# A fused decoder block: the first branch's q and k chain placed ahead of the second q's sums, both halves of a turned block sent to DRAM before either is read back, and the second branch turned behind the 21st unit

## The chip, the cores and the metric

The kernel runs on one core of a Trainium2 chip. The metric is the time of one execution in microseconds; three runs of the kernel before gave 373.08 (median), 372.19 and 373.63. Engines are called PE (matrix products), DVE (VectorE), ACT (ScalarE), POOL (GpSimd) and SP (it only issues transfers here). Each runs its own instructions in a fixed order and waits for others by semaphores.

## The reference, cut to what matters

One decoder layer on 256 tokens with 1024 channels: two attention branches of eight heads with 64 channels, a gated merge, and a gated convolutional feed-forward part.

```python
h = rms_norm(x, attn_norm_g)
qa, ka, va, qb, kb, vb, f_logit, g_logit = split(h @ w_in)
qa, ka = partial_rope(rms_norm(heads(qa), gqa)), partial_rope(rms_norm(heads(ka), gka))
o_a = softmax(causal(qa @ ka.T / 8)) @ va            # first branch: one block of 256 keys
qb, kb = rms_norm(heads(qb), gqb), rms_norm(heads(kb), gkb)
c = cumsum(log_sigmoid(f_logit + b_forget))
o_b = softmax(causal(qb @ kb.T / 8 + c[t] - c[s])) @ vb   # second branch
x = x + (gate_0 * (o_a @ w_a) + gate_1 * (o_b @ w_b)) @ w_out
u, g = split(rms_norm(x, ffn_norm_g) @ w_up)
x = x + (silu(conv3(g)) * u) @ w_down
```

## The kernel before

Every product is made of three single-pass products of rounded operands: each weight w is split into whi (rounded, ACT, line 137) and wlo = w - whi (DVE, line 138), and x likewise into xh and xl. Weights come in chunks of 1 MB, each issued by SP (line 130) into one of three buffers `raw`; a chunk has two halves, and the split of a half is called a unit here. Eight units belong to the first branch's q and k ("head"). Then follow, by the list `chunks`, units 9 to 12 for the second branch's q, 13 to 16 for its k, 17 and 18 for gate 0, 19 and 20 for gate 1, 21 to 24 for the first branch's v ("qkv", 0), 25 and 26 for gate 2, 27 to 30 for the second branch's v ("qkv", 3), then the other gates, two units each (31 and 32 gate 3, 33 and 34 gate 4, 35 and 36 gate 5). A chunk's load can start when the units of the chunk three places earlier are split, since they share a buffer.

PE's order is written by hand: first q and k (line 285), second q and k (line 299, 11 us each), gate 0, the forget logits, gate 1, the first branch's scores (line 462), the first v, gate 2, the second branch's scores, the second v, gates 3 to 5, the transposes of the probabilities, and so on to the feed-forward part. On the other engines a scheduler sets the order by program order, by priorities (`soon`, FIRST) and by edges `after(i, j)`, which only say that i stands behind j. So such an edge costs nothing of itself, but an instruction that waits holds everything behind it on its engine.

The path of q and k from projection to scores goes over several engines. `finish_qk` squares the projections on ACT, sums on DVE (line 317), takes the inverse root (`rsqrt_mean`, DVE and ACT in turn) and multiplies on DVE (line 329) into `qn` (second branch: into the tile `ol`). For the first branch POOL then turns 16 of each head's channels by the rope (lines 335 to 338). `turn_blocks` transposes 32x32 blocks on DVE (line 353), half d=1 first and then half d=0, which has the rope, and POOL issues a write of each half to DRAM, 512 KB (line 356, `blocks<-pT`). `move_blocks` reads them back in four transfers of 256 KB (line 364, `bias<-blocks`), and ACT scales them into qT and kT (lines 369 and 374; second branch: into the tile `oh`). POOL also works on the forget rows (lines 397, 412 to 415), which end in a sum over time that the second branch's bias (`forget_bias`) needs.

A pool of eight PSUM banks serves all products. The built program lets a product have a bank as soon as its last holder has been read. The sixth bank of the second branch's scores, which their third pair of heads is the first to use, is here the one from which ACT reads the first half of the first v (line 303); the second v has the banks of gate 2, which DVE's product reads (line 581), and of the first v's other half (line 305).

## Time and profile before

| | |
|---|---|
| runs | 373.08 us (372.19 to 373.63) |
| profiled execution, its own time | 373.12 us |
| its span, first to last instruction | 371.3 us |
| PE busy | 354.9 us, 96% of the span |
| DVE, ACT, POOL busy | 277.8, 222.6, 47.1 us |
| mean granted TensorE clock | 0.981 |
| moved by DMA | 72.49 MB, 195 GB/s |

The span is 1.8 us shorter than the time of the same execution; differences of spans stand for differences of times. A row of a timeline has the start and the length in us, engine, line, operation, tiles (written <- read) and shape, how often it came in a row, and in brackets how long the engine idled before it and what ended that. A row of waits has the sum, the count and the longest. A row of DMA issues has the queue, the count, KB of each and the median us from issue to landing, within the window asked for.

### The profile page before, as it was taken

To read this page: it belongs to the slowest core of one execution; us is meant where nothing else is said; L and a number is where in the kernel's file an instruction comes from. 1 tells how busy PE (TensorE), PEld (TensorE's weight loads), DVE (VectorE), ACT (ScalarE), POOL (GpSimd) and SP (SyncE) were. 2 spreads that over 40 slices of the span, in tenths; PEclk is the share of its full clock that TensorE was granted. 3 is DMA by queue.
4 is the path that set the end of the run, shared out by engine and by line. 5 is a ranking of instruction groups with operands and counts; after the bars stand their busy time and mean duration, and the time that the engine had idled before them with its cause. 6 is when DMAs were issued, how large, how long until landed. Compare 5 with 4: busy or idle time off the path is not lost.

```text
span 371.3 us, 7462 instructions
## 1 busy us (share of the span) xinstructions
PE 354.9 (96%) x3053; PEld 337.3 (91%) x3053; DVE 277.8 (75%) x475; ACT 222.6 (60%) x378; POOL 47.1 (13%) x70
## 2 busy tenths in 40 slices
PE   9999996199999999999999999999999999999995
PEld 5888885088889999999999999999999999999995
DVE  5898899585699656986779967677686867778653
ACT  5858660586999599453768645455464555545420
POOL 3532264242013000000170000000000000000000
PEclk9999999589999999999999999999999999999999
DMA  8977548976233843565464566446555545645003
GB/s 286 405 281 251 210 171 286 309 230 248 118 114 115 341 129 112 216 214 190 166 228 145 197 223 211 165 197 227 166 184 219 196 169 203 228 150 192 3 0 115
DMA packets 13347, 72.49 MB, mean 195 GB/s; under 512 B 1880, under 2 KB 3040, under 8 KB 5888
## 3 DMA queue, kind: packets, MB, share of 16 engines
q1 hardware_dynamic: 11664, 66.62, 49.7%
q0 software_dynamic: 1504, 5.38, 4.5%
q8 instruction: 24, 0.39, 0.4%
q14 instruction: 11, 0.09, 0.1%
q10 hardware_dynamic: 144, 0.00, 0.0%
HBM read 68.84 MB, written 3.15 MB: 194 GB/s over the span
## 4 chain that ended last, share of the span: by engine, by line
PE 89%; DMA 5%; POOL 2%; DVE 1%; ACT 1%; issue 1%; POOLq 0%
PE bank L571 14%; PE bank L572 14%; PE bank L573 14%; PE bank L299 9%; PE bank L285 6%; PE bank L784 5%; PE bank L785 5%; PE bank L783 5%; DMA bias<-blocks 3%; DMA blocks<-pT 2%; PE bank L707 2%; PE bank L681 2%; PE bank L709 2%; PE bank L708 2%; PE bank L683 2%; PE bank L682 2%
## 5 line engine op out<-in xcount | busy, mean ns | idle before, releaser
L138 DVE TENSOR_TENSOR wlo<-raw,whi 128x1024 fp32r<-128x1024 f32 x120 | 147.1, 1231 | 49.3 <-ACT whi L137 49.2
L137 ACT ACTIVATE whi<-raw 128x1024 fp32r<-128x1024 f32 x120 | 125.6, 1059 | 79.3 <-PE bank L572 37.1
L573 PE MATMUL bank<-oh,wlo 128*128 128x256 f32 x352 | 96.8, 275 | 0.0
L571 PE MATMUL bank<-oh,whi 128*128 128x256 f32 x352 | 96.8, 275 | 0.0
L572 PE MATMUL bank<-ol,whi 128*128 128x256 f32 x352 | 96.8, 275 | 0.0
L573 PEld LDWEIGHTS bank<-oh,wlo 128*128 128x128 f32 x352 | 66.1, 188 | 0.0
L572 PEld LDWEIGHTS bank<-ol,whi 128*128 128x128 f32 x352 | 66.1, 188 | 0.0
L571 PEld LDWEIGHTS bank<-oh,whi 128*128 128x128 f32 x352 | 66.1, 188 | 0.0
L571 PE MATMUL bank<-xh,whi 128*128 128x256 f32 x128 | 35.7, 279 | 0.0
L572 PE MATMUL bank<-xl,whi 128*128 128x256 f32 x128 | 35.3, 275 | 0.0
L573 PE MATMUL bank<-xh,wlo 128*128 128x256 f32 x128 | 35.3, 275 | 0.0
L571 PEld LDWEIGHTS bank<-xh,whi 128*128 128x128 f32 x128 | 24.0, 188 | 1.0 <-issue 0.4
L572 PEld LDWEIGHTS bank<-xl,whi 128*128 128x128 f32 x128 | 24.0, 188 | 0.1
L573 PEld LDWEIGHTS bank<-xh,wlo 128*128 128x128 f32 x128 | 24.0, 188 | 0.0
L299 PE MATMUL bank<-whi,xh 128*128 128x512 f32 x64 | 21.2, 391 | 0.0
L299 PE MATMUL bank<-whi,xl 128*128 128x512 f32 x64 | 21.0, 388 | 0.0
L299 PE MATMUL bank<-wlo,xh 128*128 128x512 f32 x64 | 21.0, 388 | 0.0
L750 DVE TENSOR_TENSOR sq<-bank,rs 128x512 f32<-128x512 f32 x22 | 15.1, 691 | 6.6 <-PE bank L573 6.5
L681 PE MATMUL bank<-oh,whi 128*128 128x256 f32 x64 | 17.6, 275 | 0.0
L682 PE MATMUL bank<-ol,whi 128*128 128x256 f32 x64 | 17.6, 275 | 0.0
L683 PE MATMUL bank<-oh,wlo 128*128 128x256 f32 x64 | 17.6, 275 | 0.0
L707 PE MATMUL bank<-xh,whi 128*128 128x256 f32 x64 | 17.6, 275 | 0.0
(197 smaller groups left out, 769.0 us busy)
## 6 DMA issues: line engine op xcount, KB each, us to landing
raw<-in_wu SPq DMA_DIRECT2D x22, 1024.0 KB, 4.8
raw<-in_wd SPq DMA_DIRECT2D x11, 1024.0 KB, 4.8
raw<-in_qkv SPq DMA_DIRECT2D x8, 1024.0 KB, 5.3
raw<-in_wg SPq DMA_DIRECT2D x8, 1024.0 KB, 5.2
raw<-in_wb SPq DMA_DIRECT2D x4, 1024.0 KB, 5.5
raw<-in_wo SPq DMA_DIRECT2D x4, 1024.0 KB, 4.8
raw<-in_head SPq DMA_DIRECT2D x6, 512.0 KB, 6.6
blocks<-pT POOLq DMA_DIRECT2D x4, 512.0 KB, 5.4
```

The source lines that it names most:

```text
L137: i = nc.scalar.activation(hi[:, s], raw[:, s], AF.Copy)
L138: d = nc.vector.tensor_tensor(lo[:, s], raw[:, s], hi[:, s].bitcast(F32), op=ALU.subtract)
L285: nc.tensor.matmul(pt[t], lhs[:, k, t * P:(t + 1) * P], rhs, start=(k == 0 and i == 0), stop=(k == KT - 1 and i == 2))
L299: nc.tensor.matmul(pt[t], lhs[:, k, t * P:(t + 1) * P], rhs[:, c], start=(k == 0 and i == 0), stop=(k == KT - 1 and i == 2))
L571: nc.tensor.matmul(o, wh[:, w], mh[:, k], start=(k == 0 and i == 0), stop=False)
L572: nc.tensor.matmul(o, wh[:, w], ml[:, k], start=False, stop=False)
L573: nc.tensor.matmul(o, wl[:, w], mh[:, k], start=False, stop=(k == KT - 1 and i == 1))
L681: nc.tensor.matmul(o, wh[:, w], oh[:, 4 * br + k], start=(k == 0), stop=False)
L682: nc.tensor.matmul(o, wh[:, w], ol[:, 4 * br + k], start=False, stop=False)
L683: nc.tensor.matmul(o, wl[:, w], oh[:, 4 * br + k], start=False, stop=(k == 3))
L707: nc.tensor.matmul(o, wh[:, w], mh[:, k], start=(k == 0 and i == 0), stop=False)
L783: nc.tensor.matmul(o, wh[:, w], ah, start=(p == 0 and h == 0 and c == 0), stop=False)
```

## The change

The first branch's q and k product goes in front of the second q's sums on DVE by an edge on these sums; some splits (units 16 and 18 on DVE, 19, 23 and 27 on ACT) get edges behind steps of q and k's chain; the reads of a turned block stand behind both writes; the second branch's transposition moves from behind gate 1's product to behind unit 21's wlo, and its reads from behind the forget rows of `forget_chain` to behind the first forget row; its scaling on ACT stands behind the second pair's softmax instead of the third's.

```diff
@@ load
+                if (c, h) == (("qkv", 0, 1), 0):
+                    after(i, moved[0])
+                if (c, h) == (("qkv", 3, 0), 0):
+                    after(i, moved[1])
+                if (c, h) in ((("qkv", 2, 1), 1), (("wg", 0), 1)):
+                    after(d, state["qn"])
+                if (c, h) == (("wg", 1), 0):
+                    after(i, state["exp"])
+                if (c, h) == (("qkv", 0, 0), 0):
+                    state["turn"] = d
@@ finish_qk
-                if br and isk:
-                    after(i, state["qn"])
+                if br:
+                    after(i, state["last"][1] if isk else state["qn"])
...
-        rsqrt_mean(f.rearrange("p m t h -> p (m t h)"), ss.rearrange("p m t h -> p (m t h)"), HD, [n * NT * NH], "qfv")
+        state["exp"] = rsqrt_mean(f.rearrange("p m t h -> p (m t h)"), ss.rearrange("p m t h -> p (m t h)"), HD, [n * NT * NH], "qfv")[1]
@@ turn_blocks, move_blocks
-            nc.gpsimd.dma_start(rd[:, c], blocks[:, c])
-        return rd, i
+            sent = nc.gpsimd.dma_start(rd[:, c], blocks[:, c])
+        return rd, i, sent
...
-                if behind is not None:
-                    after(i, behind)
+                after(i, behind)
@@ forget_a
-        nc.vector.tensor_copy(total, fp[0:NH, :S])
+        after(nc.vector.tensor_copy(total, fp[0:NH, :S]), state["turn"])
...
-        nc.gpsimd.tensor_tensor(row(1), total, rsB[:NH], op=ALU.mult)
+        fg["row"] = nc.gpsimd.tensor_tensor(row(1), total, rsB[:NH], op=ALU.mult)
@@ the main sequence
-                rd, i = turn_blocks(0, state["qn"])
-                moved.append(move_blocks(0, rd))
+                rd, i, sent = turn_blocks(0, state["qn"])
+                moved.append(move_blocks(0, rd, sent))
     catch_up(lag=1, lo=state["qn"])
-    gate(0)
+    read = gate(0)
+    after(read, state["qn"])
     with soon():
         flat_lo = forget_a()
+        rd, i, sent = turn_blocks(1, state["turn"])
+        after(fg["row"], sent)
     catch_up(lo=flat_lo)
 
     read = gate(1)
+    after(read, i)
     with soon():
         sps = scores(0)
-        rd, i = turn_blocks(1, state["last"][1])
-        after(i, read)
-        done = softmax(0, 0, sps[0], i)
+        done = softmax(0, 0, sps[0], read)
     forget_chain(done)
     with soon():
-        for pair in (1, 2):
-            softmax(0, pair, sps[pair], i)
-        last = move_blocks(1, rd, fg["z"], last_exp[0])
-        softmax(0, 3, sps[3], i, last)
+        softmax(0, 1, sps[1], read)
+        moved.append(move_blocks(1, rd, fg["row"], last_exp[0]))
+        for pair in (2, 3):
+            softmax(0, pair, sps[pair], read, moved[1])
```

In the built program PE's order and SP's are as before. PSUM banks are given out otherwise in one place: the sixth bank of the second branch's scores is now the one of gate 2, and the second v has both banks of the first v. Lines of the changed kernel are one higher than before at the splits, ten or eleven higher from `finish_qk` on. The first place is DVE, where the first branch's factor (`qf` with 32 elements) is ready to be made. Before:

```order
L230 SCALAR_TENSOR_TENSOR qfv<-qfv 128x32
L317 TENSOR_REDUCE ss<-sq 128x8
L231 TENSOR_TENSOR qfv<-qfv 128x32
L317 TENSOR_REDUCE ss<-sq 128x8
L232 SCALAR_TENSOR_TENSOR qf<-qfv 128x32
L138 TENSOR_TENSOR wlo<-raw,whi 128x1024
L322 TENSOR_TENSOR qf<-qf,rsw 128x32
L228 TENSOR_SCALAR qfv<-ss 128x16
L138 TENSOR_TENSOR wlo<-raw,whi 128x1024
L329 TENSOR_TENSOR qn<-bank,qf 128x2x4x32 x8
```

The two sums (`ss`) are the second q's, and units 16 and 17 are split ahead of qn. The same place on DVE after the change:

```order
L241 SCALAR_TENSOR_TENSOR qfv<-qfv 128x32
L242 TENSOR_TENSOR qfv<-qfv 128x32
L243 SCALAR_TENSOR_TENSOR qf<-qfv 128x32
L333 TENSOR_TENSOR qf<-qf,rsw 128x32
L340 TENSOR_TENSOR qn<-bank,qf 128x2x4x32 x8
L328 TENSOR_REDUCE ss<-sq 128x8 x2
L364 STREAM_TRANSPOSE pT<-qn 128x1024
L239 TENSOR_SCALAR qfv<-ss 128x16
L139 TENSOR_TENSOR wlo<-raw,whi 128x1024
```

The factor and all eight products now stand ahead of the sums, and the splits behind. The second place is POOL's queue from the end of the rope to the second branch's reads. Before:

```order
L356 DMA blocks<-pT 128x1024
L364 DMA bias<-blocks 32x4x512
L356 DMA blocks<-pT 128x1024
L364 DMA bias<-blocks 32x4x512 x3
L397 TENSOR_TENSOR gates<-gates,rsB 8x256
L356 DMA blocks<-pT 128x1024 x2
L412 TENSOR_TENSOR gates<-gates 8x256
L413 TENSOR_TENSOR gates<-gates 8x256
L415 TENSOR_TENSOR gates<-gates 8x256
L364 DMA bias<-blocks 32x4x512 x4
```

One read of half d=1 stands between the two writes of the first branch. POOL after the change:

```order
L367 DMA blocks<-pT 128x1024 x2
L375 DMA bias<-blocks 32x4x512 x4
L367 DMA blocks<-pT 128x1024 x2
L407 TENSOR_TENSOR gates<-gates,rsB 8x256
L375 DMA bias<-blocks 32x4x512 x4
L422 TENSOR_TENSOR gates<-gates 8x256
```

Both writes go first in each branch, and the second branch's reads stand ahead of three forget rows instead of behind them. The third place is ACT around the scaling of the second branch's q and k (`oh<-bias`). Before, with buffer numbers (whi_905 to whi_959 are units 27 to 30, s_872 the fourth pair's probabilities, bank_885 and bank_886 the first v):

```order
L137 ACTIVATE whi_921<-raw_903 128x1024
L137 ACTIVATE whi_939<-raw_937 128x1024
L137 ACTIVATE whi_959<-raw_937 128x1024
L303 ACTIVATE V_179<-bank_885,rsw_175 128x512
L369 ACTIVATE oh_180<-bias_862,gq_174 128x1024
L374 ACTIVATE oh_180<-bias_862,sm_80 128x4x64 x4
L490 ACTIVATE s_872,l_874<-s_872,nm_873 128x128
L490 ACTIVATE s_872,l_874<-s_872,nm_873 128x256
```

Units 27 to 30 and the first copy of v stand ahead of the scaling, and one pair's exponentials behind. ACT after the change:

```order
L420 ACTIVATE gates_79<-gates_79 8x256
L379 ACTIVATE oh_180<-bias_849,gq_174 128x1024
L384 ACTIVATE oh_180<-bias_849,sm_80 128x4x64 x4
L500 ACTIVATE s_859,l_861<-s_859,nm_860 128x128
L500 ACTIVATE s_859,l_861<-s_859,nm_860 128x256
L500 ACTIVATE s_859,l_861<-s_859,nm_860 128x128
L500 ACTIVATE s_859,l_861<-s_859,nm_860 128x256
L500 ACTIVATE s_872,l_874<-s_872,nm_873 128x128
L500 ACTIVATE s_872,l_874<-s_872,nm_873 128x256
L500 ACTIVATE s_872,l_874<-s_872,nm_873 128x128
L500 ACTIVATE s_872,l_874<-s_872,nm_873 128x256
L138 ACTIVATE whi_905<-raw_903 128x1024
```

The scaling moved in front of two pairs' exponentials (s_859 and s_872) and of unit 27 with all that follows it. On DVE the split of that unit stands ahead of gate 2's product, which frees the bank that the second scores wait for:

```order
L504 RECIPROCAL r_870<-l_861 128x4
L504 RECIPROCAL r_883<-l_874 128x4
L139 TENSOR_TENSOR wlo_906<-raw_903,whi_905 128x1024
L591 TENSOR_TENSOR gates_79<-bank_958,rsB_177 128x512
L139 TENSOR_TENSOR wlo_922<-raw_903,whi_921 128x1024
```

Before, gate 2's product stood behind the splits of units 27 to 30.

## The prediction

> **What bounds the kernel now.** I read the page's busy times first, then the list of who waits for whom on PE, then PE's timeline around the one long wait, and last the granted clock in short windows.

> ```profile
> span 371.3 us, 7462 instructions
> PE 354.9 (96%) x3053; PEld 337.3 (91%) x3053; DVE 277.8 (75%) x475; ACT 222.6 (60%) x378; POOL 47.1 (13%) x70
> PE bank L462 <- ACT kT L374: 11.5, 1, 11.5
> 61.15 0.28 PE L573 MATMUL bank<-xh,wlo 128*128 128x256 f32 x1
> 72.92 5.21 PE L462 MATMUL bank<-kT,qT 64*64 64x64 f32 x64 [11.49 <-ACT kT L374]
> 78.06 0.50 PE L299 MATMUL bank<-whi,xh 128*128 128x512 f32 x1
> 94.61 2.41 PE L462 MATMUL bank<-oh 64*64 64x64 f32 x64
> 96.95 0.50 PE L299 MATMUL bank<-whi,xh 128*128 128x512 f32 x1
> 64.00:65.00 1.00, 0.00 (x0) 0.52 0.98 397
> 77.00:78.00 1.00, 1.00 (x20) 0.65 0.49 197
> ```

> PE is busy for 354.9 of 371.3 us and waits for another engine once: 11.49 us, from 61.43 to 72.92, until ACT has written the first branch's kT. Everything else that PE does is back to back, so PE is the bound and this wait is what a better order can win. The wait costs more than itself. The two windows (length, PE busy, granted clock, DMA share, GB/s) show the clock at half from about 64.0, that is 2.6 us after PE fell idle, to about 77.7, 4.8 us after it resumed. So the first branch's 64 score matmuls take 78.06 - 72.92 = 5.14 us where the second branch's take 96.95 - 94.61 = 2.34. The stall is worth 11.49 + 2.80 = 14.3 us.

> **The change, part by part.** *First branch.* These rows are the chain that ends the wait: DVE, POOL, then ACT.

> ```profile
> 36.17 0.18 DVE L230 SCALAR_TENSOR_TENSOR qfv<-qfv 128x32 f32<-128x32 f32 x1
> 38.95 0.69 DVE L317 TENSOR_REDUCE ss<-sq 128x8 f32<-128x512 f32 x1 [2.60 <-ACT sq L316]
> 42.80 2.74 DVE L329 TENSOR_TENSOR qn<-bank,qf 128x256 f32<-128x256 f32 x8
> 48.52 1.21 DVE L138 TENSOR_TENSOR wlo<-raw,whi 128x1024 fp32r<-128x1024 f32 x1
> 51.47 1.25 DVE L353 STREAM_TRANSPOSE pT<-qn 128x1024 f32<-128x1024 f32 x1
> 43.97 0.46 POOL L335 TENSOR_TENSOR p<-qn,rc 128x128 f32<-128x128 f32 x1 [10.49 <-DVE qn L329]
> 48.53 1.53 POOL L335 TENSOR_TENSOR p<-qn,rc 128x128 f32<-128x128 f32 x1
> 55.95 0.55 POOL L356 DMA_DIRECT2D blocks<-pT  x1
> 61.10 1.10 POOL L364 DMA_DIRECT2D bias<-blocks  x2 [4.04 <-DMA blocks<-pT]
> 71.32 1.15 ACT L369 ACTIVATE qT<-bias,gq 128x1024 f32<-128x1024 f32 x1 [4.08 <-DMA bias<-blocks]
> blocks<-pT POOLq DMA_DIRECT2D x2, 512.0 KB, 4.3
> blocks<-pT POOLq DMA_DIRECT2D x2, 512.0 KB, 8.0
> bias<-blocks POOLq DMA_DIRECT2D x4, 256.0 KB, 4.7
> bias<-blocks POOLq DMA_DIRECT2D x2, 256.0 KB, 9.1
> ```

> At 36.35 DVE has what it needs for qn, but its next row is a sum of squares of the second q, which waits 2.60 us for ACT; behind it come the rest of qn's factor and two splits, and qn starts at 42.80. After the change the factor's three rows (0.2 each, as L230) and the eight qn rows (2.74) follow at once: qn is done at 39.8 instead of 45.5. POOL's rope is twelve rows of 0.46 like the one at 43.97; two of the twelve took about 1 us more, the one at 48.53 beside a split. From 38.2 they end at 43.7, or 44.7 with one such hold. The second transposition (d=0) then stands behind two sums (1.3), the first transposition (1.25), two splits (2.4), the second q's factor (0.9) and its four products (1.4): it runs from 46.7 to 48.0, where before it ended at 52.7. Its write is issued at 48.0, not behind the first read-back as at 55.95, but nearly 8 us earlier.

> The last four rows give the landing times: writes 4.3 us in the stretch 50 to 61 and 8.0 in 60 to 72, where weights were loading; reads 4.7 in 78 to 87 and 9.1 in 60 to 72. After the change a weight load leaves at about 49.2, behind unit 18's split, and shares the engines with this write and the reads of the other half, so I take 5.5, nearer to 4.3: landed 53.5. The two reads that wait for it are issued from there; the next load leaves behind unit 20's split (57.4), so the reads take the 4.7 and land at 58.8. The first score matmul follows 1.6 us after the landing (71.3 to 72.92): 60.4, when PE is ready at 61.43. **The wait goes whole: -14.3.** With the worse rows (8.0 and 9.1) PE would start at 67.2, 5.8 late; that is the other end.

> *Second branch.* Here the change adds a wait, since reads and scaling move in front of much of ACT's queue.

> ```profile
> 57.27 2.35 DVE L138 TENSOR_TENSOR wlo<-raw,whi 128x1024 fp32r<-128x1024 f32 x2
> 63.08 2.34 DVE L138 TENSOR_TENSOR wlo<-raw,whi 128x1024 fp32r<-128x1024 f32 x2
> 63.24 2.77 POOL L397 TENSOR_TENSOR gates<-gates,rsB 8x256 f32<-8x256 f32 x1 [1.03 <-DVE gates L396]
> 75.76 0.17 DVE L467 MEMSET bank<- 64x128 f32 x1
> 81.84 0.24 DVE L494 RECIPROCAL r<-l 128x4 f32<-128x4 f32 x2
> 89.78 0.67 ACT L303 ACTIVATE V<-bank,rsw 128x512 f32<-128x512 f32 x1
> 90.35 1.14 ACT L369 ACTIVATE oh<-bias,gq 128x1024 f32<-128x1024 f32 x1
> 92.98 0.39 ACT L490 ACTIVATE s<-s,nm 128x128 f32<-128x128 f32 x1
> 94.87 1.38 ACT L305 ACTIVATE V<-bank,rsw 64x512 f32<-64x512 f32 x2
> L137 ACT ACTIVATE whi<-raw 128x1024 fp32r<-128x1024 f32 x120 | 125.6, 1059 | 79.3 <-PE bank L572 37.1
> L138 DVE TENSOR_TENSOR wlo<-raw,whi 128x1024 fp32r<-128x1024 f32 x120 | 147.1, 1231 | 49.3 <-ACT whi L137 49.2
> ```

> Units 20 and 21 were split from 57.27, behind the second k's factor and products. That chain hangs on PE's end of k (49.1) and on ACT, and loses only the second transposition that stood ahead of it, 1.1 us of its wait: 56.2. From there DVE runs units 20 and 21 (2.4), the copy, two transpositions (2.4), gate 1's product, three 8-row sums and units 22 to 24 (3.6) bring the first score memset to 66.7. The forget row on POOL (L397) can start at 64.4, beside two splits as at 63.24, and ends at 67.3 like that one, 0.6 behind the second split. Only then come the four reads on POOL's queue, 67.3 to 69.6; nothing but the forget rows waits behind them there. They land 4.7 to 9.1 us after the last issue at 69.0: 73.7 to 78.1.

> ACT's scaling of the second q (L369) now stands behind two pairs' exponentials and three of the forget rows. Memsets and sixteen maximum rows took 81.84 - 75.76 = 6.1 us before; with unit 25 and two forget rows between them they end at 74.6, those that L369 is queued behind about 1 us earlier, and one exponential and one logarithm later L369 can start: **75.0**, from DVE's side. The reads' range brackets it; I take 75.0, and 78.1 as the other end.

> From there the queue is fixed. Scaling takes 92.98 - 90.35 = 2.6, eight exponentials twice the four from 92.98 to 94.75, 3.5, and only then comes whi of unit 27 (1.1), its wlo (1.2) and gate 2's product (0.7): 84.1. PE reaches the second scores at 61.43 + (94.61 - 78.06) + 2.34 = 80.3 and uses the bank that gate 2 held after half of them, at 81.5. So **a new wait of about 2.6 us**, 5.7 with the reads at the other end, none if ACT got there 2.6 earlier. V's copies, the first of which stood ahead of L369 before (89.78), end at 84.8 and 86.2, just in time for the value projection's two banks, which PE asks for at 85.2 and, six matmuls later, 86.6.

> *Later.* The same DVE work now has fewer idle gaps to catch up in.

> ```profile
> 98.50 1.22 DVE L440 TENSOR_TENSOR bias<-gates,cc 128x1024 f32<-128x1024 f32 x1
> 115.77 1.22 DVE L138 TENSOR_TENSOR wlo<-raw,whi 128x1024 fp32r<-128x1024 f32 x1
> 119.04 0.28 PE L571 MATMUL bank<-xh,whi 128*128 128x256 f32 x1
> ```

> Unit 31's whi follows V's copies and unit 30's, so its wlo ends at 89.5 and the bias rows start there. Before, unit 35 was split 18.5 us after that point (98.50 to 116.99); with gate 3's product (0.7) that now comes first this is 108.7. PE wants it for gate 5 at 119.04 - 11.7 = 107.3, and its low half two matmuls later, at 107.6. I count the 1.1; the other end is 0, since idle moments of DVE within the 18.5 us may close up. On SP two loads leave one to two us later, since they wait for units 16 and 18, which are now split behind the products; units 21 to 24 aren't asked for until after the first scores. All other edits only fix orders in which PE has no part: PE's own rows stand as before, and as many.

> Sum, against the profiled execution's own 373.12 us (the runs' median is 373.08): 373.12 - 14.3 + 2.6 + 1.1 = **362.5**.

> **The rivals.** *The clock falls again.* The new wait of 2.6 us is as long as PE had been idle when the clock fell before, and it came back 4.8 us after PE resumed; half of that is lost, 2.4: 364.9. Against it: 2.6 is the very edge, and the wait may be shorter. [...]

> *The second wait doesn't come.* If DVE's maxima run ahead by 2.6 us, the time is 359.9. For it: 2.6 is a small difference of two sums of over 15 us. Against it: the reads' lower end alone, 73.7, already costs 1.3.

> *The first kT stays late*, because the d=0 write meets a weight load and two splits. The case for it is in two rows.

> ```profile
> 69.75 1.18 DVE L138 TENSOR_TENSOR wlo<-raw,whi 128x1024 fp32r<-128x1024 f32 x1
> 70.12 0.55 POOL L356 DMA_DIRECT2D blocks<-pT  x1 [0.52 <-DVE pT L353]
> ```

> A write issued beside a split took its usual 0.55 to issue, but these writes landed after 8.0. With 8.0 for the write, the reads are issued at 56.0 and meet the next load; halfway to 9.1 they land at 63, and PE starts 3 us late: 365.5, up to 368.3. [...]

> *Slower, or no change.* One mechanism: the second branch's reads hold up ACT. PE's value projection starts 10.2 us after L369, and before it started at 96.95; the gain is gone when L369 starts at 86.8, reads landing 17.8 us after the last issue. The longest landing shown is 9.1, so this needs twice that. That the change doesn't do what it says I exclude, since the built orders show both moves.

> **How the numbers follow.** The forecast has 0.50, the clock 0.13, no second wait 0.14, a late first kT 0.17, no change 0.03, slower 0.03. The range 359.0 to 367.0 leaves out the last two and the late end of the fourth. About 0.5% (1.9 us) is what a measurement of this kernel can tell from no change; all but the last two cases are faster by more: 0.94, 0.03, 0.03.

> **What would show it.** Right: the list of waits has no kT wait of over 2 us at the first scores; qn ends near 39.8; the second scores wait 2 to 3 us for gate 2's product, with unit 27's whi just ahead on ACT; the clock row has no half-speed stretch near 65. Wrong: a first wait left and reads of over 6 us (the third rival), L369 of the second branch far from 75.0, or a wait of PE for a split near 107.

## The result and the profile after

The changed kernel takes 368.08 us (median of 4 runs, 367.6 to 369.03) against 372.63 for the kernel before in the same session: a ratio of 0.9879, 95% interval 0.9847 to 0.9912. The profiled execution took 367.6 us. So the change gains 4.5 us where 10.6 were forecast, and the time lies above the forecast's range.

The page's head and the list of what PE waits for, changed kernel:

```profile
span 365.8 us, 7460 instructions
PE 354.7 (97%) x3053; PEld 337.2 (92%) x3053; DVE 278.3 (76%) x475; ACT 221.9 (61%) x378; POOL 46.3 (13%) x70
PE bank L472 <- DVE gates L591: 4.1, 1, 4.1
PE bank L472 <- ACT kT L384: 1.2, 2, 0.9
PE bank L581 <- DVE nm L496: 0.9, 1, 0.9
```

The wait of 11.49 us is nearly gone, as forecast. A wait of 4.1 for gate 2's product took its place, where 2.6 was forecast, and one of 0.9 that the forecast doesn't have: gate 3's first matmul waits for the maxima (`nm`) of the second branch's softmax. The timeline of the changed kernel shows where these lie (start, length, and in brackets the idle time before and what ended it):

```profile
36.88 2.74 DVE L340 TENSOR_TENSOR qn<-bank,qf 128x256 f32<-128x256 f32 x8
48.65 0.54 POOL L367 DMA_DIRECT2D blocks<-pT  x1 [2.58 <-DVE pT L364]
53.16 1.09 POOL L375 DMA_DIRECT2D bias<-blocks  x2 [1.83 <-DMA blocks<-pT]
60.45 1.15 ACT L379 ACTIVATE qT<-bias,gq 128x1024 f32<-128x1024 f32 x1 [7.96 <-DMA bias<-blocks]
62.05 0.27 PE L472 MATMUL bank<-kT,qT 64*64 64x64 f32 x2 [0.87 <-ACT kT L384]
64.72 2.25 POOL L375 DMA_DIRECT2D bias<-blocks  x4
65.47 0.49 PE L310 MATMUL bank<-whi,xh 128*128 128x512 f32 x1
78.39 1.15 ACT L379 ACTIVATE oh<-bias,gq 128x1024 f32<-128x1024 f32 x1 [3.33 <-DMA bias<-blocks]
85.62 1.23 DVE L139 TENSOR_TENSOR wlo<-raw,whi 128x1024 fp32r<-128x1024 f32 x1 [0.77 <-ACT whi L138]
86.76 0.68 DVE L591 TENSOR_TENSOR gates<-bank,rsB 128x512 f32<-128x512 f32 x1
87.50 0.66 PE L472 MATMUL bank<-oh 64*64 64x64 f32 x4 [4.06 <-DVE gates L591]
90.57 2.36 DVE L139 TENSOR_TENSOR wlo<-raw,whi 128x1024 fp32r<-128x1024 f32 x2 [0.46 <-ACT whi L138]
92.85 1.22 DVE L450 TENSOR_TENSOR bias<-gates,cc 128x1024 f32<-128x1024 f32 x1
102.40 0.35 PE L581 MATMUL bank<-xh,whi 128*128 128x256 f32 x1 [0.90 <-DVE nm L496]
122.22 0.38 PE L581 MATMUL bank<-xh,whi 128*128 128x256 f32 x1
```

The last two rows have these counterparts before the change, in PE's timeline:

```profile
108.05 0.36 PE L571 MATMUL bank<-xh,whi 128*128 128x256 f32 x1
127.72 0.38 PE L571 MATMUL bank<-xh,whi 128*128 128x256 f32 x1
```

The first value projection starts 12.59 us earlier than before (65.47 for 78.06). At gate 3 5.65 of that are left (102.40 for 108.05), at the next gate 5.50, and 5.5 at the end. So the stretch from 65 to 102 gives 6.9 us back. In it DVE stands idle twice for 0.77 and 0.46 from unit 27's split on, and hardly at all (gaps under 0.1) in the 9.6 us ahead of gate 3.

The granted clock in that stretch (windows of the changed kernel: length, the engines' busy times with PE first, then the clock, DMA share and GB/s):

```profile
84.20:87.60 3.40, 0.10 (x4) 0.10 (x8) 2.16 (x4) 3.40 (x6) 0.00 (x0) 1.00 0.54 222
87.70:91.00 3.30, 3.30 (x33) 2.56 (x30) 2.75 (x5) 3.24 (x5) 0.00 (x0) 0.50 0.36 132
```

The rival of the falling clock came true: after the 4.06 us it is at half for 3.4 us. The transfers of the two branches, from the lists of DMA issues in the windows 48 to 56 and 62 to 68 (KB each, median us from issue to landing):

```profile
bias<-blocks POOLq DMA_DIRECT2D x4, 256.0 KB, 6.7
blocks<-pT POOLq DMA_DIRECT2D x1, 512.0 KB, 4.2
...
bias<-blocks POOLq DMA_DIRECT2D x4, 256.0 KB, 11.5
```

The reads took 6.7 and 11.5, where 4.7 and at most 9.1 were forecast.

### The profile page after: what moved, and what is told of

It reads as the page before. It is cut to its first block, busy times and chain, and to the rows that moved or that the text cites. A ratio compares the mean times of both kernels' runs of the same rounds, so it can differ in the third digit from the quotient of the medians.

```text
span 365.8 us, 7460 instructions
## 1 busy us (share of the span) xinstructions
PE 354.7 (97%) x3053; PEld 337.2 (92%) x3053; DVE 278.3 (76%) x475; ACT 221.9 (61%) x378; POOL 46.3 (13%) x70
## 4 chain that ended last, share of the span: by engine, by line
PE 71%; DVE 9%; DMA 6%; issue 6%; ACT 4%; POOL 1%; SPq 1%; DVEq 0%; POOLq 0%; ACTq 0%
PE bank L581 14%; PE bank L583 13%; PE bank L582 13%; PE bank L794 5%; PE bank L796 5%; PE bank L795 5%; DMA bias<-blocks 3%; DVE wlo L139 3%; PE bank L719 2%; PE bank L693 2%; PE bank L720 2%; PE bank L718 2%; PE bank L694 2%; PE bank L692 2%; ACT whi L138 2%
## 5 line engine op out<-in xcount | busy, mean ns | idle before, releaser
L138 ACT ACTIVATE whi<-raw 128x1024 fp32r<-128x1024 f32 x120 | 125.0, 1058 | 61.6 <-PE bank L582 37.1
## 6 DMA issues: line engine op xcount, KB each, us to landing
raw<-in_head SPq DMA_DIRECT2D x6, 512.0 KB, 6.6
blocks<-pT POOLq DMA_DIRECT2D x4, 512.0 KB, 4.3
```

Of the source, the lines that this page charges most:

```text
L138: i = nc.scalar.activation(hi[:, s], raw[:, s], AF.Copy)
```

## The experiments

Three times order all runs: F, the start of the first value projection; T, the start of the second branch's scaling on ACT; G, gate 3's first matmul. From G to the end of the span all runs take 263.2 to 265.0 us, so little differs there but the clock. PE's own work from F to G is 29.99 us, as before the change (78.06 to 108.05, no wait).

| run | F | T | G | G - T | G - F | span | time |
|---|---|---|---|---|---|---|---|
| before | 78.06 | 90.35 | 108.05 | 17.70 | 29.99 | 371.3 | 372.63 |
| changed kernel | 65.47 | 78.39 | 102.40 | 24.01 | 36.93 | 365.8 | 368.08 |
| e1 scaling last | 69.03 | 78.32 | 102.05 | 23.73 | 33.02 | 367.0 | 368.82 |
| e2 splits first | 67.91 | 80.28 | 101.86 | 21.58 | 33.95 | 366.8 | 368.54 |
| e3 product first | 68.25 | 77.90 | 101.85 | 23.95 | 33.60 | 366.7 | 368.48 |
| e4 later loads held | 66.25 | 75.26 | 99.28 | 24.02 | 33.03 | 364.2 | 366.04 |
| f1 first load held | 63.68 | 81.47 | 105.88 | 24.41 | 42.20 | 369.2 | 371.05 |
| f2 both held | 63.48 | 77.92 | 102.41 | 24.49 | 38.93 | 365.7 | 367.43 |
| f3 first branch only | 67.52 | 91.39 | 109.14 | 17.75 | 41.62 | 372.3 | 374.20 |
| f4 rows in front | 63.83 | 78.49 | 105.20 | 26.71 | 41.37 | 369.9 | 371.72 |
| g1 split behind | 67.12 | 76.13 | 100.65 | 24.52 | 33.53 | 365.3 | 368.00 |
| g2 splits early | 65.83 | 77.66 | 98.73 | 21.07 | 32.90 | 362.6 | 365.29 |
| g4 read between | 71.92 | 78.95 | 103.79 | 24.84 | 31.87 | 367.1 | 368.79 |
| s1 second branch only | 74.88 | 83.30 | 107.33 | 24.03 | 32.45 | 372.3 | 373.41 |

Times of e1 to f4 are single executions (the kernel before beside them: 373.44 and 373.48), g1 to g4 medians of 4, s1 of 10. Executions of one kernel lie up to 3.6 us apart (g1: 366.76 to 370.33), so the times of single executions alone tell little here; F, T, G and the span belong to the one execution that was profiled. Line numbers shift by some lines from kernel to kernel.

**Three orders of the same work.** The first theory was that the 4.06 us come from ACT's queue: scaling stands 3.33 us for its reads, with eight exponentials and unit 27's whi behind it. e1 moves scaling behind the exponentials:

```diff
-        moved.append(move_blocks(1, rd, fg["row"], last_exp[0]))
+        back = move_blocks(1, rd, fg["row"])
         for pair in (2, 3):
-            softmax(0, pair, sps[pair], read, moved[1])
+            softmax(0, pair, sps[pair], read)
+        moved.append(scale_blocks(1, back, last_exp[0]))
...
     read = gate(2)
+    after(wlos[("qkv", 3, 0), 1], read)
```

> The second branch's reads stay where the change put them, but its five scaling instructions stand behind the exponentials of pairs 2 and 3 instead of in front of them; gate 2's product stays right behind unit 27's split. Theory order (the loss sits in ACT's queue: eight exponentials and unit 27's whi wait behind a scaling that waits 3.3 us for its reads): the exponentials run from 75.1 to 78.6, scaling from 78.6, unit 27's whi from 81.3, gate 2's product ends at 84.2 instead of 87.45; the wait at the second scores falls from 4.06 to about 0.7, the clock stays up there, and the span is 361 to 363 instead of 365.8. Theory throughput (ACT and DVE have no time left, whatever the order): the 5 us come out at another place and the span stays within 1 us of 365.8. Theory place (gate 2's product is late only because it stands behind unit 27's split on DVE): gains here too, so the third run tells it apart.

e2 splits units 27 to 29 first, by dropping unit 27's edge behind the scaling and putting the scaling behind unit 27's whi:

```diff
-                    after(i, moved[1])
+                    state["u27"] = i
...
+        moved.append(scale_blocks(1, back, state["u27"]))
+    for i in exps[8:]:
+        after(i, moved[1])
```

> Units 27 to 29 are split ahead of the second branch's scaling; the exponentials of pairs 2 and 3 stay behind the scaling. Theory order: these splits fit into the 3.3 us in which ACT waits for the reads, scaling still starts near 78.4, gate 2's product runs as soon as PE is done with gate 2 (82.0 to 82.7) and the wait for it is gone; V's copies still stand behind the exponentials (84.6), end at 85.3 and 86.6 and cost 1 to 1.5 us in front of the value projection: span 361.5 to 363.5. Theory throughput: within 1 us of 365.8.

e3 puts gate 2's product ahead of unit 27's split on DVE:

```diff
     read = gate(2)
+    after(state["lo27"], read)
```

> On DVE gate 2's product stands in front of unit 27's split; ACT's queue is as in the changed kernel up to V's copies. Theory place: the wait of 4.06 goes and nothing else is late, span 361 to 362. Theory order: the wait of 4.06 at the second scores goes, but V's first copy still ends at 88.06 behind scaling, eight exponentials and three splits; PE asks for its bank at 84.4 and waits 3 to 3.7 us there: span 364.5 to 366.

Rows of e1's timeline, and of e3's:

```profile
102.05 0.47 PE L586 MATMUL bank<-xh,whi 128*128 128x256 f32 x1 [2.98 <-ACT whi L139]
```

```profile
77.90 1.15 ACT L381 ACTIVATE oh<-bias,gq 128x1024 f32<-128x1024 f32 x1 [1.94 <-DMA bias<-blocks]
101.85 0.58 PE L583 MATMUL bank<-xh,whi 128*128 128x256 f32 x1 [3.02 <-ACT V L316]
```

All three took away the wait for gate 2's product (e2 kept 1.23 us there, for ACT's copies of V), and none gained: spans of 366.7 to 367.0. PE came to gate 3 earlier and waited there instead, 3.0, 2.1 and 3.0 us. The theory of ACT's queue is down, and so is that of the product's place, by these single executions; "throughput" comes nearest, though it expected 365.8 within 1 and e1 lies 1.2 above it. The three runs also show that the first branch's reads land anew each time: F is 2.4 to 3.6 us later than in the profiled execution of the changed kernel, with the same edits in front of it, and that didn't show at G.

**Taking the loads away from the reads.** e4 holds SP's loads of units 27 to 30 until the second branch's reads have landed, by a small transfer that depends on them:

```diff
+                    if c == ("qkv", 3, 0):
+                        after(loads[c], state["held"])
...
+        if br:
+            state["held"] = nc.sync.dma_start(dr.tile([P, 16], F32, name="hold"), moved[:, 0:16])
```

> The weight loads of units 27 to 30, which before left at 63.56 and 67.00, are held on SP behind a small transfer that reads what the second branch's four reads brought, so that no load runs beside these reads. Theory contention (the reads issued from 64.7 to 67.0 landed at 78.3 because two 1 MB loads shared the DMA engines): the reads land 4.7 to 6 us after the last issue, by 73, scaling starts at 75.1 as soon as ACT is free, gate 2's product ends at 84.2, the wait falls from 4.06 to about 0.7, span 361 to 363. Theory slow reads (they need 11 us by themselves, as POOL's queue or one slow engine gives them): they land near 78 again and the span stays within 1 us of 365.8.

Two rows of e4's timeline, and its reads in the window 62 to 68.5:

```profile
75.26 1.14 ACT L383 ACTIVATE oh<-bias,gq 128x1024 f32<-128x1024 f32 x1
99.28 0.36 PE L585 MATMUL bank<-xh,whi 128*128 128x256 f32 x1 [2.85 <-DVE nm L500]
```

```profile
bias<-blocks POOLq DMA_DIRECT2D x4, 256.0 KB, 5.0
```

Contention is shown: without the loads the reads take 5.0 instead of 11.5 us, and scaling starts when ACT is free. The two other runs in which both loads were held until these reads had landed, f2 and g1, have 4.9 and 4.9. Beside the loads there is no fixed price: in e1, e2 and e3, where they weren't held, the same reads took 6.2, 9.0 and 7.5. From the first read's issue to the last landing all four took 7.3 to 7.5 us in e4, f2 and g1, and 9.9 to 13.6 in e1 to e3 and the changed kernel. The span of 364.2 misses the 361 to 363 that went with this theory, for G follows T, not PE: T is 3.13 earlier than in the changed kernel, and G 3.12. That gave the second theory, a chain from T to gate 3's bank of 24.0 us over ACT's and DVE's queues.

f1 holds the load of units 23 and 24, which left at 49.5, behind the first branch's reads in the same way (`("qkv", 0, 1)`), and f2 does both; edges keep the other queues in the changed kernel's order.

> On SP the load of units 23 and 24, which left at 49.5 beside the first branch's reads, is held until these reads have landed (a small transfer behind them on SP waits for them); three edges keep the other queues in the changed kernel's order. Theory load in front of the reads (the first two reads, issued at 50.2, land at 57 and 58 because they share the DMA engines with that 1 MB load, and the two d=0 reads queue behind them): the first reads now land at 54 to 55, the d=0 reads, issued at 53.2, by 58, the first scores start without a wait at 61.2 to 61.5 and take 2.4, and the first value projection starts at 63.6 to 63.9 instead of 65.5 to 69. If the load has no part in it, the d=0 reads land at 60.4 or later again. On the end: theory chain (gate 3 starts 24.0 us after the second branch's scaling, as it did in the changed kernel, 78.39 to 102.40, and in the run with held loads, 75.26 to 99.28, since DVE's queue of splits, bias rows and maxima is full from there; PE's wait at the second scores is slack of that chain): scaling starts near 78 again, gate 3 near 102, span within 1 us of 365.8. Theory waits (PE's end follows its waits one by one): the first value projection's gain comes through, span 363.3 to 364.

> Both holds together: the load of units 23 and 24 behind the first branch's reads, those of units 27 to 30 behind the second branch's. Theory chain: scaling starts at 75.1 to 75.5, as in the run with the second hold alone, gate 3 24.0 later, at 99.1 to 99.5, and PE, which is earlier by 2 to 3 us, only waits longer there; span 363 to 364.5, no better than the 364.2 of the second hold alone. Theory waits: the two gains add, span 361 to 362.3.

Four rows of f1's timeline, then its transfers in the windows 48 to 56 and 58 to 66:

```profile
61.34 2.41 PE L486 MATMUL bank<-kT,qT 64*64 64x64 f32 x64
63.68 0.50 PE L315 MATMUL bank<-whi,xh 128*128 128x512 f32 x1
81.47 1.15 ACT L386 ACTIVATE oh<-bias,gq 128x1024 f32<-128x1024 f32 x1 [4.90 <-DMA bias<-blocks]
105.88 0.39 PE L597 MATMUL bank<-xh,whi 128*128 128x256 f32 x1 [0.55 <-ACT V L319]
```

```profile
bias<-blocks POOLq DMA_DIRECT2D x4, 256.0 KB, 4.4
...
raw<-in_qkv SPq DMA_DIRECT2D x2, 1024.0 KB, 7.7
blocks<-pT POOLq DMA_DIRECT2D x2, 512.0 KB, 11.5
```

Here the first branch does all that was forecast of it and more: no wait, scores in 2.34, F at 63.68. The reads that took 6.7 take 4.4. And the kernel is 3.4 us of span slower: the held loads now run beside the second branch's writes (11.5 us instead of 4.4), T slips to 81.47 and G with it. The theory of the chain had expected T near 78 here and at 75.1 to 75.5 in f2 (it was 77.92), so its spans missed too (369.2 and 365.7), as did those of the theory of waits. Given the T that was measured, the chain still holds (24.41, and 24.49 in f2), and the theory of waits doesn't: F is 1.8 and 2.0 us earlier than in the changed kernel, and G isn't earlier. In the changed kernel's execution POOL's reads took 6.7 and 11.5 us beside SP's loads, 2.3 and 6.5 more than in f1 and e4 without them.

**Half of the change.** f3 has the first branch's edits alone, with the second branch turned, read and scaled where it was before; s1 has the second branch's alone. The fences show a part of each edit.

```diff
-        rd, i, sent = turn_blocks(1, state["turn"])
-        after(fg["row"], sent)
...
+        rd, i, sent = turn_blocks(1, state["last"][1])
+        after(i, read)
...
+        for pair in (1, 2):
+            softmax(0, pair, sps[pair], i)
+        last = move_blocks(1, rd, fg["z"], last_exp[0])
+        softmax(0, 3, sps[3], i, last)
```

> The change's edits of the first branch alone; the second branch's transpositions, reads and scaling stand where they were before the change (behind unit 24's split, behind the forget gate's rows, behind V's copies). Theory waits: reads issued near 70 to 80 land by 84 to 88, scaling starts at 86 to 90, PE waits 5 to 9 us at the second scores; span 367.5 to 371, so the second half of the change is worth 2 to 5 us. Theory chain: before the change gate 3 followed the scaling by at most 17.7 us (90.35 to 108.05) since the splits stood ahead of it, so gate 3 starts at 102 to 105 here, span 365.5 to 368: the second half of the change is worth about nothing.

```diff
-                if br:
-                    after(i, state["last"][1] if isk else state["qn"])
+                if br and isk:
+                    after(i, state["qn"])
...
-                moved.append(move_blocks(0, rd, sent))
+                moved.append(move_blocks(0, rd, None))
```

> The change's edits of the second branch alone; up to the first branch's scaling every queue stands as before the change. Theory two chains (gate 3 starts at whichever is later: 30.0 us after the first value projection, by PE's own work, or 24.0 us after the second branch's scaling, by ACT's and DVE's queues): the first value projection starts at 78 as before, and the scaling, which needs the tile that the first branch's scaling frees at 74 and stands behind the exponentials of pairs 0 and 1, starts at 82 to 84, so both chains end at 106 to 108.5: span 370 to 372 (before: 371.3), median within 2 us of before's 373. Theory sum (the two halves of the change contribute their own gains, and the first half alone gave none): the second half brings the whole of it, median 367 to 369.

A wait and two rows of f3, then two rows of s1's timeline:

```profile
PE bank L470 <- ACT oh L382: 8.9, 1, 8.9
91.39 1.15 ACT L377 ACTIVATE oh<-bias,gq 128x1024 f32<-128x1024 f32 x1 [1.89 <-DMA bias<-blocks]
109.14 0.28 PE L579 MATMUL bank<-xh,whi 128*128 128x256 f32 x1
```

```profile
83.30 1.15 ACT L374 ACTIVATE oh<-bias,gq 128x1024 f32<-128x1024 f32 x1 [6.08 <-DMA bias<-blocks]
107.33 0.36 PE L576 MATMUL bank<-xh,whi 128*128 128x256 f32 x1 [2.42 <-DVE nm L491]
```

Each half alone gives nothing: 374.20 beside 373.48 for f3, a single execution, and a ratio of 1.0017 (0.9994 to 1.0041) for s1. Together they give 4.5. In f3 the second branch isn't ready: T stays at 91.39, and the wait of 11.49 comes back as 8.9 at the second scores; both theories had put f3 too low. In s1 PE is bound by the first wait (8.2), reaches gate 3 at 104.91, 30.03 after F, and then waits for the chain, which ends 24.03 after T. F had been expected at 78 as before and came at 74.88: the first branch's last two reads left at 60.25 (before: 61.10) and the next two weight loads only from 65.31 on (before: 61.14). That this made the reads land earlier is not shown by a run. Before the change the second branch's lateness was hidden behind the first wait, with 2.7 us to spare: the first part of kT is ready 1.6 after T, as f3 shows (91.39 to 92.99), so at 92.0, and PE asked for it at 94.61.

**What the order of the two writes is worth.** g4 reads the d=1 half back before the d=0 half is written:

```diff
-                after(i, behind)
+                after(i, behind if br else sents[1 - d])
+            if not br and d:
+                after(sents[1], i)
```

> In the first branch the d=1 half is read back before the d=0 half is written, as before the change; everything else is the changed kernel. Theory load in front: the d=1 reads land at 57 to 58 in any case, behind the load of units 23 and 24, and the d=0 reads follow each other at 1.1 us; with the d=0 write issued at 51.3 instead of 48.6 its reads leave at 55.5 to 56 and land 4.5 to 5 us later, at 60 to 61: no change, span and median within 1 us of the changed kernel's (365.8; 368.1). Theory order of the transfers (writing both halves first brings kT as much earlier as the write is issued earlier): the d=0 reads land at 63 to 64, the first value projection starts 2.5 us later and scaling of the second branch shifts by less; median 369 to 371.

Four rows of its timeline:

```profile
66.48 0.88 PE L476 MATMUL bank<-kT,qT 64*64 64x64 f32 x6 [5.18 <-ACT kT L388]
71.92 0.67 PE L311 MATMUL bank<-whi,xh 128*128 128x512 f32 x1
78.95 1.14 ACT L383 ACTIVATE oh<-bias,gq 128x1024 f32<-128x1024 f32 x1
103.79 0.36 PE L585 MATMUL bank<-xh,whi 128*128 128x256 f32 x1 [1.68 <-ACT ol L504]
```

This tells the two theories of the end apart most sharply. A wait of 5.18 us is back at the first scores and F is 6.45 later than in the changed kernel, 2.9 to 4.0 later than in e1 to e3, so the order of the transfers does matter for kT (the theory of the load in front missed there): the d=0 write, issued at 51.23 instead of 48.65, took 7.6 us instead of 4.2. The end is 1.3 us of span later, and the median 368.79 instead of 368.08: PE's wait was mostly slack of the other chain. Not wholly, since F also acts on that chain. Of the 1.39 us that G is later, 0.56 are T's, which had no wait for its reads; and behind T DVE stood 1.32 us until PE was through with gate 2.

**Shortening the chain.** The fences show a part of each edit. f4 puts the bias rows in front of units 30 and 31's splits, units 27 and 28 in front of the scaling, with the first hold and one load of the second; g1 is e4 with unit 32's split behind the maximum that frees gate 3's bank; g2 splits units 27 and 28 ahead of the scaling, 29 behind the exponentials, leaves the rows where they were, has g1's late split, and holds only the load of units 29 and 30.

```diff
+        rows = forget_bias(wlos[("qkv", 3, 1), 0])
+        after(wlos[("qkv", 3, 1), 1], rows)
```

> The first hold, and of the second only that of the load of units 29 and 30; units 27 and 28 are split ahead of the second branch's scaling, so that DVE does them in the 5 to 9 us in which it stood idle ahead of unit 27's split; gate 2's product comes behind the scan; and the five bias rows go in front of units 30 and 31's splits. Theory chain: with 2.4 us of DVE's queue moved into its idle time and the rows not waiting for ACT's splits, gate 3 starts at 96 to 98.5, and the span is 358 to 361.5. Theory ACT (ACT has no idle moment from 75 to 103 either, so what is put in front only delays what is behind): gate 3 starts no earlier than 99, span 363 or more.

```diff
+    after(parts[("wg", 3), 1][1], maxima[20])
     gate(3)
```

> As the run with the loads of units 27 to 30 held (span 364.2, there gate 3 waited 2.85 us for its bank, and the clock was at half for 3.4 us), and unit 32's split, which stood on DVE between the second branch's second and third maximum, goes behind the fifth, the one that frees gate 3's bank; PE needs that split only 2.7 us into gate 3. Theory chain (DVE's queue ends in gate 3's bank): that bank comes free 1.2 us earlier, so gate 3 starts 22.8 instead of 24.0 us after the second branch's scaling, the wait falls to 1.6, and if that is short enough for the clock to stay up, 1.6 us more: span 361 to 363. If gate 3 waits for something else: within 0.5 us of 364.2.

```diff
+                if (c, h) in ((("qkv", 3, 0), 0), (("qkv", 3, 0), 1)):
+                    after(i, exps[7])
...
+    after(parts[("qkv", 3, 0), 0][0], fg["r"])
+    with soon(FIRST):
+        moved.append(scale_blocks(1, back, parts[("qkv", 3, 0), 1][0]))
+    for i in exps[8:]:
+        after(i, moved[1])
+    after(parts[("qkv", 3, 1), 0][0], exps[-1])
```

> Only the load of units 29 and 30 is held; units 27 and 28 are split ahead of the second branch's scaling and unit 29's split comes behind the exponentials; gate 2's product stands behind the scan, the bias rows behind unit 31's split as in the changed kernel, and unit 32's split behind the fifth maximum of the second branch. Theory chain: the splits of units 27 and 28 move into DVE's idle time, 76 to 82, so that its queue behind the second branch's scaling is 3.6 us shorter than in the changed kernel; with scaling near 77 gate 3 starts at 97.5 to 98.5, without a wait of over 1.5 us, and the span is 360 to 362. Theory ACT (what is put in front of scaling on ACT delays what is behind it, V's copies and units 30 and 31, by the same): gate 3 starts at 99.5 or later and the span is 363 or more.

The first bias row in f4 and in g1, and two rows of g2's timeline:

```profile
93.58 1.22 DVE L472 TENSOR_TENSOR bias<-gates,cc 128x1024 f32<-128x1024 f32 x1 [5.93 <-DMA gates<-cd]
```

```profile
92.23 1.23 DVE L457 TENSOR_TENSOR bias<-gates,cc 128x1024 f32<-128x1024 f32 x1 [1.56 <-DMA gates<-cd]
```

```profile
79.41 1.19 DVE L143 TENSOR_TENSOR wlo<-raw,whi 128x1024 fp32r<-128x1024 f32 x1
98.73 0.36 PE L597 MATMUL bank<-xh,whi 128*128 128x256 f32 x1 [0.86 <-DVE nm L509]
```

f4 and g1 failed at the same place: the rows need the sums over time, which come by two transfers, and DVE waited 5.93 and 1.56 us for the second. `cd` took 5.1 and 5.0 us from issue to landing where it took 1.9 in the changed kernel, and `gates<-cd` 5.1 and 6.3 instead of 4.9; that they meet the loads that were held is my estimate, which no run shows by itself. In f4 the sums were late besides: `cd` left at 82.74 instead of 79.61, where ACT had split units 27 and 28 (74.16 to 76.15) ahead of its last two forget rows. f4's span lies where the theory of ACT had put it, 363 or more. g1's median is 368.00 (366.76 to 370.33), no gain over the changed kernel. g2, where these splits stand behind ACT's last forget row (`fg["r"]`), did what was expected of the chain, 21.07 instead of 24.0, with unit 27's split at 79.41 in DVE's idle time and not at 85.62. It changes several places at once, and no run shows how much each is worth; it has no stretch at half clock there (mean granted clock 0.998), and takes 365.29 us (364.36 to 365.77): 0.9793 of the kernel before (0.9767 to 0.9819), better than both kernels. Its span of 362.6 lies 0.6 above what was expected, gate 3 by 0.2.

## Why the prediction was wrong

**The first branch: right in its steps, late by a load.** qn was done at 39.6 (forecast 39.8), the d=0 write was issued at 48.65 (48.0) and took 4.2 (5.5). The terms listed for the second transposition add up to 47.05, not to the 46.7 that was carried on, which is 0.35 of the 0.65. The reads were to take 4.7 and took 6.7: I let the weight load at 49.2 slow the write, but the d=1 reads left right behind that load, at 50.20 and 50.76, and landed at 56.96 and 58.03; the d=0 reads, issued at 53.16 and 53.70, landed behind them at 59.12 and 60.43. f1, without that load, has 4.4. F was to be 63.77 and was 65.47. PE waited 0.87 and 0.36, and up to 2.83 in runs with the same edits in front of it (e1). None of this set the end.

**The second branch: the step that failed is the start of its scaling.** The prediction took 75.0 with 78.1 as the other end; it was 78.39. DVE's side came as worked out (ACT was ready at 75.06); the reads, taken to land 4.7 to 9.1 us after their issue, took 11.5 beside two loads of 1 MB, so they landed at 78.28 although they were issued from 64.72 on and not from 67.3. That the loads held them up is what e4 shows. From there each link of the forecast held: gate 2's product 9.1 after the scaling (87.45), bias rows 14.5 after it (92.85).

**The sum: a link was left out.** I followed that chain only to gate 2's product, added PE's wait there, and asked for DVE's lag next at unit 35 (1.1). But the same queue runs on through the bias rows into the maxima that free gate 3's bank. The fifth maximum, before the change and after it:

```profile
107.82 0.07 DVE L486 DVE_READ_ACCUMULATOR2_ANT nm<- 128x1 f32 x1
102.18 0.07 DVE L496 DVE_READ_ACCUMULATOR2_ANT nm<- 128x1 f32 x1
```

It ended 0.16 us ahead of gate 3 before the change and 0.15 after it, and in both gate 3 started 9.55 us after the first bias row (98.50 to 108.05, 92.85 to 102.40). So there was nothing to spare on this path before either, and the rows of the kernel before could show it. The forecast puts the bias rows at 89.5 and gate 3 at 108.05 - 14.3 + 2.6 = 96.35, only 6.85 behind them; with 9.55 its own terms give 99.05, which is 2.7 later. Counted from scaling, the forecast has 21.35, and measured are 24.0. So of the 6.05 us that gate 3 came later, 3.39 are the late scaling and 2.66 the rest of the chain. The 1.1 at unit 35 didn't come, and 0.15 were lost behind gate 3: 6.05 - 1.1 + 0.15 = 5.1, the miss from 362.5 to 367.6.

**The rivals.** The clock fell again, but the 1.7 us or so that it takes (half of the 3.41 us at half, 87.60 to 91.02) lie inside the chain: in e4 it fell later (3.4 us at half), PE waited 2.85 at gate 3 instead, and G - T is the same. The late first kT came true by 1.23 us of waiting, but not by its write, which took 4.2 us beside a weight load and two splits; the reads were late. The slower case had the right mechanism, reads that hold up ACT, and put the point of no gain at a scaling that starts at 86.8; by T + 24.0 it is 84.05, since 108.05 was gate 3's start before. What no rival had is that the two branches are two chains of which the later one counts. With the changed kernel's order behind the scaling, gate 3 starts about at the later of F + 30.0 and T + 24.0: for the changed kernel 95.5 and 102.4, for g4 101.9 and 103.0 (measured 103.79), for s1 104.9 and 107.3. Other orders have another length from T on (21.07 in g2, 26.71 in f4). The first of the two was the later one only before the change, so its side of the rule rests on PE's work being the same. By this rule a gain on F beyond T - 6 is worth nothing.

**Open.** Which link of the 24.0 us binds isn't one thing: what arrived last at gate 3 was DVE's maxima in the changed kernel, e4, f4, g1, g2 and s1, ACT's copies or exponentials in e2, e3, f1, f2 and g4, and ACT's split of a weight in e1; in e1 the chain was no shorter although the exponentials had moved ahead of T. An earlier `cd` transfer, and less work on ACT between T and G, weren't tried.

## What to carry to other kernels

Removing the longest wait of the bound engine is worth only what the next chain to the same point leaves; work out when each chain ends there, over every engine's queue and not just to the first bank that it frees, and take the later. Test it by making one chain later: g4 lost 6.45 us on one and 1.3 at the end. And a transfer that is moved earlier lands among others: its duration belongs to the place, not to the transfer (the same four reads took 4.9 to 11.5 us).

## What the hardware showed that wasn't expected

The clock went to half after PE waits as short as 1.24 and 0.36 us together (e2) and stayed up after one of 2.69 (g1). Windows of both (columns as above):

```profile
61.00:64.60 3.60, 1.93 (x25) 1.34 (x27) 2.80 (x5) 3.28 (x6) 0.62 (x2) 1.00 1.01 413
64.70:68.00 3.30, 3.30 (x51) 2.41 (x43) 2.78 (x5) 3.30 (x5) 2.79 (x5) 0.50 0.93 282
```

```profile
59.20:62.60 3.40, 1.81 (x16) 1.61 (x15) 2.98 (x5) 0.50 (x1) 1.11 (x2) 1.00 1.01 276
62.60:66.00 3.40, 1.87 (x40) 1.45 (x44) 1.32 (x3) 3.40 (x7) 0.72 (x1) 1.00 0.87 357
```

The four reads of a branch land one after the other: with the loads held, their last parts came at 69.6, 70.7, 71.8 and 72.8 in e4, 1.0 to 1.1 us apart. A read lands in 16 parts. In the changed kernel 15 parts of the last read had landed at 75.2 and the sixteenth at 78.28, which is what ACT waited for. So late a last part belongs to that execution: it came 0.9, 0.8 and 0.0 us behind the fifteenth in e1, e2 and e3, where the reads were slow all the same (their last parts at 76.92, 78.61 and 77.80).
